# Gated blocks kept as float32 between two stages of a hybrid attention / DeltaNet layer, with a re-measured instruction plan

## The chip, the cores and the metric

The kernel runs on one core of a Trainium2 chip. A core has a matrix engine (PE, whose weight loads are listed apart as PEld), a vector engine (DVE), an activation engine (ACT), a general engine (POOL) and 16 DMA engines, fed here from one queue of the sync engine (SP). Each engine runs its own instructions strictly in order and waits on semaphores for the others. The metric is the device time of one execution in microseconds (us).

## The reference

One layer of a flow-matching backbone: modulated RMSNorm, attention and gated DeltaNet heads side by side, an output projection, and a gated MLP with a depthwise convolution of width 3. The change lies in the MLP, which reads

```python
def conv_ffn(h, w_up, conv_w, conv_b, w_down):
    u = depthwise_conv(h @ w_up, conv_w) + conv_b
    gate, val = jnp.split(u, 2, axis=-1)
    return (jax.nn.silu(gate) * val) @ w_down
```

with h of 2048 tokens x 1024, w_up 1024 x 5632, w_down 2816 x 1024, all float32. The layer's result then passes a last RMSNorm.

## The kernel before

The last part of the program (from L1563) does the output projection, the up stage (h @ w_up, convolution, gate) and the down stage (@ w_down). Nothing in it runs in the order in which it is written: the function `flow` is executed once against a recording object (`Plan`, L195, with `Flow`, L2332, for this part), which notes every instruction and what it depends on, gives each a duration from `cost` (L229), simulates the five engines with a greedy list scheduler (`order`, L307) and then issues the instructions in the simulated order (`issue`, L402). From there that order is fixed on each engine; waits are real. All recorded instructions therefore carry one line number, L407, and are told apart by the names of their tiles.

Float32 accuracy on the matrix engine is got by splitting a float32 tile into two float16 halves, a high part (an ACT cast) and a low part (a subtraction of the high part from the original), and by running three float16 products for one (`PAIRS`, L1581; `split`, L1628):

```python
def split(lo_e, hi, lo, src):
    S.copy(out=hi, in_=src)
    lo_e.tensor_tensor(out=lo, in0=src, in1=hi, op=ALU.subtract)
```

On top of it, up and down products use a 2 x 2 block scheme with seven products in place of eight (Strassen's, in Winograd's form). The operands of the seven products are blocks and combinations of blocks: A11, S2, S1, A12, S3, A22, S4 on the weight side and B11, T2, T1, B21, T3, T4, B22 on the token side.

**Up stage.** 22 column blocks j, each for two halves of the tokens (sb 0 and 1), make 44 steps. A step has seven products of 12 matmuls (`P1` to `P7`, L1954 to L1986), summed in three PSUM banks: ua, ub and uc. The bank ub is read three times in a step (once as u, twice as a row of the tile xa), and the next product that adds to ub may start only once DVE has read it: these are the waits of "PE ub" for "DVE xa". When a step's rows are complete, `after` (L2003) runs the convolution: per row one ACT instruction and two DVE scalar_tensor_tensor instructions on the tile cv, so four of those stand together on DVE; then SiLU on ACT and the gating product on DVE. Blocks B11, T1 come from the column blocks 0 to 10, and T2, T3, B21, B22, T4 are formed when the partner block j + 11 is done. Each of the seven 128 x 512 results is split (`stored`, L1998), with the low part on DVE or POOL, and its float16 pair goes to the DRAM tensor hidc. For the next j, `scales` (L1747) and `parts_of` (L1787) prepare the weights ws_u out of raw_u: seven splits with the low part on POOL, two sums on DVE and two on POOL.

**Down stage.** 14 entries e (seven products, two token halves), each of 4 x 33 matmuls pdn on the 11 pairs hid. `load_hid` (L2058) reads an entry's pairs with two DMA transfers, two entries ahead, into four rotating tiles `ol`. `prep` (L2074) reads w_down (rd), combines up to four blocks of it on DVE and splits them (wd) for the next product; the sums usum, the residual xp / xq and the norm sums nacc_f are DVE work, too, and `last_norm` (L2240) writes finished tokens (fin).

Of the kernel before, what the change touches and what calls it, by code (L numbers as in the profile page):

```python
# [180 lines left out]
class Planned:  # L181
    def __init__(self, eng):
        self.eng, self.calls, self.dur, self.move, self.turns = eng, [], 0.0, 0.0, False
        self.deps, self.behind, self.allocs = set(), set(), []
# [10 lines left out]
class Plan:  # L195
    LAG = dict(PE=200.0, S=250.0, V=170.0, G=170.0, SY=60.0)
    TILE = 14.0
    ISSUED, SEEN = 1275.0, 930.0
# [63 lines left out]

    def add(self, eng, fn, name, kw):
# [38 lines left out]
        op.dur += d  # L302
        op.move, op.turns = max(op.move, a), "transpose" in name and eng == "SY"
# [3 lines left out]
    def order(self, weights):  # L307
# [28 lines left out]
        moved = 0.0  # L336
# [14 lines left out]
        for _ in range(n):  # L351
# [24 lines left out]
            start[i], free[e], end[i] = t, t + o.dur, t + o.dur  # L376
# [48 lines left out]
def kernel(  # L425
# [23 lines left out]
    hidc = dram.tile([2, 7, P, NJ // 2, 2, 512], F16, name="hidc")  # L449
# [1127 lines left out]
    CVW, DTAIL = 1544, ("T1", "T2", "T3", "T4", "B22")  # L1577
# [17 lines left out]
    def flow(plan):  # L1595
# [7 lines left out]
        hidd = plan.wrap(hidc, [2, 7, P, HJ, 2, 512], F16)  # L1603
# [7 lines left out]
        tailc = kept([P, 5, HJ, 2], F16, "tailc")  # L1611
# [175 lines left out]
        def parts_of(j):  # L1787
# [16 lines left out]
            G.tensor_tensor(out=a21, in0=a11, in1=a21, op=ALU.subtract)  # L1804
# [5 lines left out]
            G.tensor_tensor(out=a12, in0=a12, in1=s, op=ALU.subtract)  # L1810
# [187 lines left out]
        def stored(sb, n, j, lo_e, src, z):  # L1998
            z = z.bitcast(F16).rearrange("p (f t) -> p f t", f=2)
            split(lo_e, z[:, 0], z[:, 1], src)  # L2000
            SY.dma_start(out=hidd[sb, BLK.index(n), :, j], in_=z)

        def after(s):  # L2003
# [20 lines left out]
            if not high:  # L2024
                b11, b12 = held[sb] = hold(sb, m)
                V.tensor_tensor(out=b11, in0=c[:, lo], in1=v[:, lo], op=ALU.mult)
# [4 lines left out]
                stored(sb, "B11", m, V, b11, c[:, 0:512])  # L2031
                V.tensor_tensor(out=b11, in0=b12, in1=b11, op=ALU.subtract)
                stored(sb, "T1", m, G, b11, c[:, 512:1024])
                yield
                return
            t1, t3 = held[sb]
# [4 lines left out]
            V.tensor_tensor(out=t1, in0=b22, in1=t1, op=ALU.subtract)  # L2041
            yield
            stored(sb, "T2", m, G, t1, v[:, 1032:1544])
            V.tensor_tensor(out=t3, in0=b22, in1=t3, op=ALU.subtract)
            stored(sb, "T3", m, G, t3, mk(s3, [P, 512], F32, "junk", f"zt3_{m}_{sb}", 1))
            stored(sb, "B21", m, V, b21, c[:, 0:512])
            yield
            V.tensor_tensor(out=b21, in0=b21, in1=t1, op=ALU.subtract)
            stored(sb, "B22", m, V, b22, c[:, 512:1024])
            stored(sb, "T4", m, V, b21, c[:, 1024:1536])  # L2050
# [7 lines left out]
        def load_hid(e):  # L2058
            if e >= len(entries):
                return  # L2060
            p, sb = entries[e]
            n = ORDER[p][1]
            hids[e] = []
            for a, w in ((0, 8), (8, HJ - 8)):
                t = mk(ol3, [P, 8, 2, 512], F16, "ol", f"hid_{e}_{a}", 4)[:, 0:w]
                SY.dma_start(out=t, in_=hidd[sb, BLK.index(n), :, a:a + w])
                if not sb and n in DTAIL:
                    V.tensor_copy(out=t[:, :, :, 511], in_=tailc[:, DTAIL.index(n), a:a + w, :])
                hids[e] += [t[:, j] for j in range(w)]
# [49 lines left out]
        def tails():  # L2119
            e5 = kept([P, 5, HJ], F32, "ends5")  # L2120
# [5 lines left out]
            split(V, tailc[:, :, :, 0], tailc[:, :, :, 1], e5)  # L2126
# [49 lines left out]
        for n, (j, sb) in enumerate(steps):  # L2176
# [15 lines left out]
            elif (j, sb) == (NJ - 1, 0):  # L2192
                drain(work)
                work = scale_wd()
            elif (j, sb) == (NJ - 1, 1):
                drain(work)
                load_hid(0)
                work = prep(0)
# [19 lines left out]
        load_hid(1)  # L2218
# [45 lines left out]
        for e, (p, sb) in enumerate(entries):  # L2264
# [3 lines left out]
            load_hid(e + 2)  # L2268
# [139 lines left out]
```

## Time and profile before

| | us |
|---|---|
| median of 3 runs | 3285.61 (3281.2 to 3290.55) |
| the profiled execution, its own time | 3282.11 |
| its span, first to last instruction | 3280.3 |
| PE busy, of the span | 3073.7 |
| DVE busy | 2407.5 |
| ACT busy | 1775.7 |
| POOL busy | 1722.1 |
| the first up product starts at | 1960.7 |
| the up products give way to the down products at | 2867 |
| the down products end at | about 3267 |

Three places are worked on below: 1960 to 2867 us (up), the boundary around 2867 us, and 2867 to 3267 us (down). A row of the view of waits says which engine stood still for which. A row of the groups of instructions gives count, busy time and mean duration of one, then how long the engine had been idle before them. A row of the windows gives, for a stretch of time, the busy time and number of instructions of PE, PEld, DVE, ACT and POOL, the granted PE clock, and the busy share of the DMA engines with their GB/s.

### The profile page before, as it was taken

The numbers are of one execution on the slowest core, as the hardware profiler recorded it, in microseconds if no ns is written. First come the engines' busy times: TensorE is split into PE (matmuls) and PEld (weight loads), VectorE is DVE, ScalarE is ACT, GpSimd is POOL, SyncE is SP. The second block draws the span as 40 slices with busy tenths as digits, with TensorE's granted clock in tenths as the row PEclk, the third lists the DMA queues.
The fourth block names the chain that finished last, engine by engine and source line by source line (L and its number), as shares of the span: only waits on it lengthen the run. The fifth ranks groups of instructions, "written<-read, shape, count | busy, mean of one in ns | idle before, by whom it ended". The sixth has DMA issues, their size and how long they took to land. (4 is left out here: it accounts for less than half of the span.)

```text
span 3280.3 us, 63243 instructions
## 1 busy us (share of the span) xinstructions
PE 3073.7 (94%) x25298; PEld 1961.1 (60%) x25298; DVE 2407.5 (73%) x3610; ACT 1775.7 (54%) x2947; POOL 1722.1 (52%) x1351
## 2 busy tenths in 40 slices
PE   6899999978999999999997998999999999999998
PEld 3789978865667777777774543444444444444445
DVE  5766486877877777788875688887887888863455
ACT  4534234346787777777776455555555555541211
POOL 4786465555887776776776344554554555200000
PEclk8899999988999999999998999999999999999999
DMA  6322344671112222333325464222222222585696
GB/s 240 91 69 88 109 129 126 177 197 36 55 44 75 67 82 82 105 118 109 104 67 219 178 246 144 74 84 90 90 89 92 93 85 75 186 302 195 234 308 209
DMA packets 280328, 423.65 MB, mean 129 GB/s; under 512 B 23144, under 2 KB 167112, under 8 KB 276944
## 3 DMA queue, kind: packets, MB, share of 16 engines
q1 hardware_dynamic: 278080, 414.19, 37.7%
q0 software_dynamic: 1952, 5.42, 0.6%
q8 instruction: 198, 3.24, 0.4%
q14 instruction: 98, 0.80, 0.1%
HBM read 284.15 MB, written 135.81 MB: 128 GB/s over the span
## 5 line engine op out<-in xcount | busy, mean ns | idle before, releaser
L407 POOL TENSOR_TENSOR lp<-p,hp 128x1024 f16<-128x1024 f32 x288 | 620.4, 2162 | 208.2 <-DVE hp L407 83.3
L407 PEld LDWEIGHTS <-ws_u 128*128 128x128 f16 x3696 | 365.0, 99 | 491.6 <-issue 73.4
L407 DVE TENSOR_REDUCE mx<-sm 128x2 f32<-128x1024 f32 (+1 forms) x320 | 356.4, 1114 | 94.7 <-PE sm L407 91.5
L407 PE MATMUL pdn<-hid,wd 128*128 128x512 f16 (+1 forms) x1980 | 400.8, 365 | 0.0
L407 ACT ACTIVATE p<-sc 128x1024 f32<-128x1024 f32 x288 | 295.2, 1025 | 127.6 <-PE sc L407 123.7
L407 DVE SCALAR_TENSOR_TENSOR cv<-xa,ufw,cv 128x1025 f32<-128x1025 f32 (+1 forms) x176 | 284.6, 1664 | 56.5 <-ACT cv L407 56.2
L407 PEld LDWEIGHTS <-wd 128*128 128x128 f16 x1980 | 193.8, 98 | 204.7
L407 PE MATMUL sc<-q,kh 128*128 128x512 f16 x576 | 220.6, 383 | 6.3 <-ACT p L407 5.9
L407 PE MATMUL sc<-qx,kx 128*128 128x512 f16 x576 | 220.3, 383 | 0.0
L407 POOL TENSOR_TENSOR ws_u<-raw_u,ws_u 128x512 f16<-128x512 f32 x110 | 191.2, 1754 | 50.5 <-ACT ws_u L407 50.5
L407 POOL TENSOR_TENSOR cv<-hold,cv 128x512 f16<-128x512 f32 x44 | 61.3, 1393 | 274.3 <-ACT cv L407 252.5
L407 ACT CAST hp<-p 128x1024 f16<-128x1024 f32 x192 | 201.0, 1047 | 3.7
L407 POOL TENSOR_TENSOR nrc_f<-nrc_f,mhalf 128x8 f32<-128x8 f32 x3 | 4.9, 1636 | 360.3 <-DVE nrc_f L407 360.3
L407 PE MATMUL ops<-vst,hp 128*128 128x65 f16 (+1 forms) x4608 | 191.9, 193 | 1.3 <-ACT hp L407 1.1
L407 PE MATMUL ua<-blk_a,ws_u 128*128 128x512 f16 x792 | 181.7, 379 | 0.7 <-ACT s L407 0.7
L407 PEld LDWEIGHTS <-hp 128*128 128x128 f16 x4608 | 164.9, 97 | 21.0 <-issue 6.9
L407 PE MATMUL po<-ol,ws_o 128*128 128x512 f16 x768 | 175.1, 385 | 1.0 <-DVE ws_o L407 1.0
L407 PE MATMUL ub<-blk_T,ws_u 128*128 128x512 f16 x528 | 129.4, 397 | 29.2 <-DVE xa L407 29.2
L531 PE MATMUL pg<-hl,ws_g 128*128 128x512 f32 x384 | 152.8, 398 | 0.0
L533 PE MATMUL pg<-hl,ws_g 128*128 128x512 f32 x384 | 152.3, 397 | 0.0
L532 PE MATMUL pg<-hl,ws_g 128*128 128x512 f32 x384 | 151.7, 395 | 0.0
L407 ACT CAST t<-pa 128x512 f16<-128x512 f32 x216 | 124.6, 583 | 43.2 <-PE pa L407 39.4
(713 smaller groups left out, 7916.4 us busy)
## 6 DMA issues: line engine op xcount, KB each, us to landing
rd<-in_wd SPq DMA_DIRECT2D x70, 512.0 KB
hidc<-cv SPq DMA_DIRECT2D x132, 256.0 KB
hid<-hidc SPq DMA_DIRECT2D x14, 2048.0 KB
raw_u<-in_wu SPq DMA_DIRECT2D x44, 512.0 KB
tk<-gsc SPq DMA_DIRECT2D x34, 512.0 KB
tT<-gsc SPq DMA_DIRECT2D x66, 256.0 KB
wm<-in_wm SPq DMA_DIRECT2D x64, 256.0 KB
gsc<-kd SPq DMA_DIRECT2D x64, 256.0 KB
```

The source lines that it names most:

```text
L407: fn(**{k: v.get() if isinstance(v, Lazy) else v for k, v in kw.items()})
L531: PE.matmul(out=ps, lhsT=hi_l(k), rhs=hi_r(k), start=st, stop=False)
L532: PE.matmul(out=ps, lhsT=hi_l(k), rhs=lo_r(k), start=False, stop=False)
L533: PE.matmul(out=ps, lhsT=lo_l(k), rhs=hi_r(k), start=False, stop=en)
```

## The change

1. **Storage.** hidc holds the seven blocks as float32 (same bytes). `stored` no longer splits; it writes one, two or three neighbouring blocks with one transfer. The up stage loses 154 ACT casts, 88 low parts on DVE and 66 low parts on POOL, and its transfers into hidc go from 154 to 88. T2, T3 and T4 are now written into the cv tile and go out together.
2. **Down stage.** `load_hid` becomes a generator that brings an entry in six pieces (five of two blocks, one of one) into two landing places, which lie in the unused part of the second `ol` tile, and splits each: one ACT cast and one DVE subtraction, 128 x 1024 for five pieces and 128 x 512 for the sixth. It runs one entry ahead. The last-column corrections (tailc) are patched piecewise in float32.
3. **Weights.** The two sums of `parts_of` that POOL did go to DVE (44 instructions of 128 x 512).
4. **Plan.** The last plan gets other fixed costs (150 ns on DVE and 140 ns on ACT, formerly 65 and 50, and 60 for 65 where a DVE instruction takes a scalar from a tile) and a rule by which a DVE and a POOL instruction that both work on SBUF with at least 128 elements slow each other down to 0.58 of their speed. `prep(0)` and the first `load_hid` start at other steps.

The core of the diff:

```diff
-    hidc = dram.tile([2, 7, P, NJ // 2, 2, 512], F16, name="hidc")
+    hidc = dram.tile([2, 7, P, NJ // 2, 512], F32, name="hidc")
...
+            d, port = o.dur, self.PORT
+            if o.port:
+                x = "G" if e == "V" else "V"
+                over = max(0.0, ported[x] - t)
+                d = d / port if d / port <= over else d + (1.0 - port) * over
+                if over:
+                    free[x] = max(free[x], ported[x] + (1.0 / port - 1.0) * min(over, d))
+                ported[e] = t + d
+            start[i], free[e], end[i] = t, t + d, t + d
...
-            G.tensor_tensor(out=a21, in0=a11, in1=a21, op=ALU.subtract)
+            V.tensor_tensor(out=a21, in0=a11, in1=a21, op=ALU.subtract)
...
-            G.tensor_tensor(out=a12, in0=a12, in1=s, op=ALU.subtract)
+            V.tensor_tensor(out=a12, in0=a12, in1=s, op=ALU.subtract)
...
-        def stored(sb, n, j, lo_e, src, z):
-            z = z.bitcast(F16).rearrange("p (f t) -> p f t", f=2)
-            split(lo_e, z[:, 0], z[:, 1], src)
-            SY.dma_start(out=hidd[sb, BLK.index(n), :, j], in_=z)
+        def stored(sb, n, j, src):
+            i = DBLK.index(n)
+            k = src.shape[1] // 512
+            SY.dma_start(out=hidd[sb, i:i + k, :, j].rearrange("n p t -> p n t"), in_=src.rearrange("p (n t) -> p n t", n=k))
...
-            hids[e] = []
-            for a, w in ((0, 8), (8, HJ - 8)):
-                t = mk(ol3, [P, 8, 2, 512], F16, "ol", f"hid_{e}_{a}", 4)[:, 0:w]
-                SY.dma_start(out=t, in_=hidd[sb, BLK.index(n), :, a:a + w])
+            t = [mk(ol3, [P, 8, 2, 512], F16, "ol", f"hid_{e}_{a}", 4) for a in range(2)]
+            hids[e] = [t[j // 8][:, j % 8] for j in range(HJ)]
+            for i, j0 in enumerate(range(0, HJ, 2)):
+                w = min(2, HJ - j0)
+                a = 3 + 2 * (i % 2)
+                land = t[1][:, a:a + w].rearrange("p j f t -> p (j f t)").bitcast(F32).rearrange("p (j t) -> p j t", j=w)
+                SY.dma_start(out=land, in_=hidd[sb, DBLK.index(n), :, j0:j0 + w])
...
+                split(V, o[:, :, 0, :], o[:, :, 1, :], land)
...
-            load_hid(e + 2)
+            coming = load_hid(e + 1)
...
+    plan.fixed = (150, 60, 0, 140, 42)
```

**DVE in the up stage, around one convolution.** This is the second token half of column block 5, which is a low block. Names: cv is the convolution's pair of tiles, xa the rows read out of PSUM, ws_u and raw_u the weights of the next block in the making, rows and hold places for gated blocks. Before:

```order
L407 TENSOR_TENSOR ws_u_1_32915<-raw_u_1_32768 128x512
L407 SCALAR_TENSOR_TENSOR cv_1_0_32917<-xa,ufw_32259,cv_1_0_32917 128x1025
L407 SCALAR_TENSOR_TENSOR cv_1_1_32920<-xa,ufw_32259,cv_1_1_32920 128x1025
L407 SCALAR_TENSOR_TENSOR cv_1_0_32917<-xa,ufw_32259,cv_1_0_32917 128x1025
L407 SCALAR_TENSOR_TENSOR cv_1_1_32920<-xa,ufw_32259,cv_1_1_32920 128x1025
L407 TENSOR_TENSOR ws_u_1_32915<-ws_u_1_32915,raw_u_0_32729 128x512
L407 TENSOR_TENSOR ends<-cv_1_0_32917,cv_1_1_32920 128x1
L407 TENSOR_TENSOR hold_32978<-cv_1_0_32917,cv_1_1_32920 128x512
L407 TENSOR_TENSOR rows<-cv_1_0_32917,cv_1_1_32920 128x512
L407 TENSOR_TENSOR xa<-ub_0_32817,s_16_0_32830 128x512
```

And now:

```order
L422 SCALAR_TENSOR_TENSOR cv_1_0_32733<-xa,ufw_32115,cv_1_0_32733 128x1025
L422 SCALAR_TENSOR_TENSOR cv_1_1_32735<-xa,ufw_32115,cv_1_1_32735 128x1025
L422 SCALAR_TENSOR_TENSOR cv_1_0_32733<-xa,ufw_32115,cv_1_0_32733 128x1025
L422 SCALAR_TENSOR_TENSOR cv_1_1_32735<-xa,ufw_32115,cv_1_1_32735 128x1025
L422 TENSOR_TENSOR ws_u_1_32789<-raw_u_1_32572 128x512
L422 TENSOR_TENSOR ends<-cv_1_0_32733,cv_1_1_32735 128x1
L422 TENSOR_TENSOR cv_1_0_32733<-cv_1_0_32733,cv_1_1_32735 128x512
L422 TENSOR_TENSOR rows<-cv_1_0_32733,cv_1_1_32735 128x512
L422 TENSOR_TENSOR xa<-ub_0_32633,s_16_0_32646 128x512
```

The first weight sum (ws_u out of raw_u alone) has moved from ahead of the four convolution instructions to behind them, and the second (ws_u out of ws_u and raw_u) to behind the read of ub.

**POOL at the same place**, the low parts and sums of that weight block, before:

```order
L407 TENSOR_TENSOR ws_u_0_32913<-raw_u_0_32729,ws_u_0_32913 128x512
L407 TENSOR_TENSOR raw_u_1_32768<-raw_u_0_32729,raw_u_1_32768 128x512
L407 TENSOR_TENSOR ws_u_0_32913<-ws_u_1_32915,ws_u_0_32913 128x512
L407 TENSOR_TENSOR ws_u_0_32913<-raw_u_0_32729,ws_u_0_32913 128x512
L407 TENSOR_TENSOR ws_u_1_32915<-raw_u_1_32768,ws_u_1_32915 128x512 x2
L407 TENSOR_TENSOR raw_u_0_32729<-raw_u_0_32729,ws_u_1_32915 128x512
L407 TENSOR_TENSOR ws_u_0_32913<-ws_u_1_32915,ws_u_0_32913 128x512
L407 TENSOR_TENSOR ws_u_1_32915<-raw_u_0_32729,ws_u_1_32915 128x512
```

And now:

```order
L422 TENSOR_TENSOR ws_u_0_32750<-raw_u_0_32407,ws_u_0_32750 128x512 x2
L422 TENSOR_TENSOR ws_u_0_32750<-ws_u_1_32789,ws_u_0_32750 128x512
L422 TENSOR_TENSOR ws_u_1_32789<-raw_u_1_32572,ws_u_1_32789 128x512
L422 TENSOR_TENSOR ws_u_0_32750<-ws_u_1_32789,ws_u_0_32750 128x512
L422 TENSOR_TENSOR ws_u_1_32789<-raw_u_1_32572,ws_u_1_32789 128x512
L422 TENSOR_TENSOR ws_u_1_32789<-raw_u_0_32407,ws_u_1_32789 128x512
```

The two raw_u sums are gone from POOL; its third instruction now reads the weight sum (ws_u_1_32789) that DVE makes behind the four convolution instructions.

**SP's queue in the down stage**, where entry 11 is loaded and the weights of the last product (rd) stream in. Before:

```order
L407 DMA hid_0_38215<-hidc 128x8192
L407 DMA rd_4_1_38218<-in_wd 128x4x256
L407 DMA out<-fin_3_38049 128x3x511
L407 DMA out<-fin_3_38049 128x3x1
L407 DMA hid_8_38236<-hidc 128x3072
```

And now:

```order
L422 DMA hid_1_38003<-hidc 128x1024 x2
L422 DMA rd_4_1_38023<-in_wd 128x4x256
L422 DMA x1c<-xq_37885 128x512
L422 DMA xp_38030<-x1c 128x3x512
L422 DMA rd_6_1_38046<-in_wd 128x4x256
L422 DMA out<-fin_3_37801 128x3x511
L422 DMA out<-fin_3_37801 128x3x1
L422 DMA out<-fin_6_37991 128x2x511
L422 DMA out<-fin_6_37991 128x2x1
L422 DMA hid_1_38003<-hidc 128x1024
L422 DMA xq_38097<-x1c 128x512
L422 DMA hid_1_38003<-hidc 128x1024
```

Two large transfers have become six, of which two start at once and the others stand between weights, residuals and output, each behind the split that empties its landing place.

More of the change, by code (lines that the diff above doesn't have):

```diff
@@ L183, in __init__ @@
         self.eng, self.calls, self.dur, self.move, self.turns = eng, [], 0.0, 0.0, False
-        self.deps, self.behind, self.allocs = set(), set(), []
+        self.deps, self.behind, self.allocs, self.port = set(), set(), [], False
 class PlanEngine:
@@ L261, in cost, with shares @@
         return 46 + n * 1.05, 0.0
+    @staticmethod
+    def shares(eng, name, kw):
+        if eng not in "VG" or name.startswith("dma_start") or name in ("tensor_reduce", "memset"):
+            return False
+        return not any(isinstance(x, Lazy) and x.root.psum for x in kw.values()) and int(np.prod(kw["out"].shape[1:])) >= 128
     def add(self, eng, fn, name, kw):
@@ L302, in add @@
         op.dur += d
+        op.port = self.shares(eng, name, kw)
         op.move, op.turns = max(op.move, a), "transpose" in name and eng == "SY"
@@ L335, in order @@
         free = dict.fromkeys(self.LAG, 0.0)
-        moved = 0.0
+        moved, ported = 0.0, dict(V=0.0, G=0.0)
         pool = {e: [] for e in free}
@@ L1602, in flow @@
         h2 = [plan.wrap(h2c[i], [P, KT, 512], F32) for i in range(NCH)]
-        hidd = plan.wrap(hidc, [2, 7, P, HJ, 2, 512], F16)
+        hidd = plan.wrap(hidc, [2, 7, P, HJ, 512], F32)
         spare = plan.wrap(rows, [P, R_END], F32)
@@ L1610, in flow @@
         ogate = kept([P, KT], F32, "ogate")
-        tailc = kept([P, 5, HJ, 2], F16, "tailc")
+        tailc = kept([P, 5, HJ], F32, "tailc")
         ends = kept([P, 4, HJ], F32, "ends")
@@ L2024, in after @@
             if not high:
-                b11, b12 = held[sb] = hold(sb, m)
-                V.tensor_tensor(out=b11, in0=c[:, lo], in1=v[:, lo], op=ALU.mult)
+                t1, b12 = held[sb] = hold(sb, m)
+                b11 = c[:, lo]
+                V.tensor_tensor(out=b11, in0=b11, in1=v[:, lo], op=ALU.mult)
                 V.tensor_tensor(out=b12, in0=c[:, hi], in1=v[:, hi], op=ALU.mult)
@@ L2030, in after @@
                 yield
-                stored(sb, "B11", m, V, b11, c[:, 0:512])
-                V.tensor_tensor(out=b11, in0=b12, in1=b11, op=ALU.subtract)
-                stored(sb, "T1", m, G, b11, c[:, 512:1024])
+                stored(sb, "B11", m, b11)
+                V.tensor_tensor(out=t1, in0=b12, in1=b11, op=ALU.subtract)
+                stored(sb, "T1", m, t1)
                 yield
                 return
-            t1, t3 = held[sb]
+            t1, b12 = held[sb]
             b21, b22 = v[:, lo], v[:, hi]
@@ L2119, in tails @@
         def tails():
-            e5 = kept([P, 5, HJ], F32, "ends5")
+            e5 = tailc
             V.tensor_tensor(out=e5[:, 0], in0=ends[:, 1], in1=ends[:, 0], op=ALU.subtract)
@@ L2294, in flow @@
                                               stop=k == HJ - 1 and f == 2, skip_group_check=True)
+                        next(coming, None)
                         if c0 == 0:
@@ L2343, in cost @@
             return Plan.cost(eng, name, kw, rate, fixed)
-    flow(Flow(tc, psn, pt3, ps3))
+    plan = Flow(tc, psn, pt3, ps3)
+    plan.fixed = (150, 60, 0, 140, 42)
+    flow(plan)
     p3.close()
```

33 lines of the change are left out of this document (15 added, 18 removed).

## The prediction

> **What bounds the kernel now.** I read the windows first, by stage, then the chain of waits, then who kept PE waiting. The windows are the start of the up stage, its steady part, its end, and the down stage (columns: window, length, then busy us and count of PE, PEld, DVE, ACT, POOL, then PE clock, DMA share, GB/s):
>
> ```profile
> 1960.50:2042.00 81.50, 70.93 (x333) 32.26 (x332) 68.20 (x80) 45.84 (x71) 33.61 (x20) 0.94 0.40 139
> 2042.00:2760.00 718.00, 671.57 (x3313) 306.03 (x3311) 595.30 (x782) 408.68 (x703) 374.50 (x238) 0.98 0.25 87
> 2760.00:2867.00 107.00, 100.06 (x457) 45.07 (x458) 88.32 (x121) 53.12 (x91) 33.22 (x21) 0.97 0.44 150
> 2867.00:3268.00 401.00, 400.03 (x2013) 197.53 (x2011) 205.47 (x311) 94.93 (x140) 9.14 (x6) 1.00 0.74 255
> ```
>
> In the down stage PE is never idle, at full clock: nothing can be won there, only lost. The chain of waits gives PE's real pace, and the windows of the tiles ua, ub, uc (PE's count first) and uns say how much there was to do:
>
> ```profile
> 2867.11 265.47 PE pdn L407 x1230
> ...
> 2042.00:2760.00 718.00, 196.45 (x857) 40.74 (x71) 0.98 0.25 87
> ...
> 2042.00:2760.00 718.00, 303.40 (x1284) 71.25 (x105) 0.98 0.25 87
> ...
> 2042.00:2760.00 718.00, 187.64 (x840) 47.81 (x70) 0.98 0.25 87
> ...
> 2042.00:2760.00 718.00, 17.67 (x332) 6.08 (x36) 4.00 (x36) 0.98 0.25 87
> ```
>
> 265.47 / 1230 = 0.2158 us per matmul. The steady part holds 857 + 1284 + 840 = 2981 of them (ua, ub, uc), 643.3 us of work, and 17.7 us of weight norms (uns): 661.0 of 718 us. So **57 us are lost**. PE's waits there:
>
> ```profile
> PE ub L407 <- DVE xa L407: 34.6, 15, 2.9
> PE uns L407 <- ACT junk L407: 9.5, 9, 2.1
> PE ub L407 <- POOL ws_u L407: 1.7, 1, 1.7
> ```
>
> 45.8 us are waits; the other 11 (671.57 busy less 661.0) are products at less than full pace, in a part whose clock averages 0.98. What makes xa late is seen in the timeline around the longest wait (start, duration, what):
>
> ```profile
> 2424.94 1.16 POOL L407 TENSOR_TENSOR ws_u<-raw_u,ws_u 128x512 f16<-128x512 f32 x1 [2.81 <-ACT ws_u L407]
> 2426.06 1.28 POOL L407 TENSOR_TENSOR raw_u<-raw_u,raw_u 128x512 f32<-128x512 f32 x1
> 2427.73 1.71 POOL L407 TENSOR_TENSOR ws_u<-ws_u,ws_u 128x512 f16<-128x512 f32 x1 [0.39 <-ACT ws_u L407]
> 2429.40 6.33 POOL L407 TENSOR_TENSOR ws_u<-raw_u,ws_u 128x512 f16<-128x512 f32 x3
> ...
> 2426.04 8.68 DVE L407 SCALAR_TENSOR_TENSOR cv<-xa,ufw,cv 128x1025 f32<-128x1025 f32 x4 [0.97 <-ACT cv L407]
> 2434.64 1.64 DVE L407 TENSOR_TENSOR ws_u<-ws_u,raw_u 128x512 f32<-128x512 f32 x1
> ...
> 2436.88 1.75 DVE L407 TENSOR_TENSOR rows<-cv,cv 128x512 f32<-128x512 f32 x1
> 2438.55 0.68 DVE L407 TENSOR_TENSOR xa<-ub,s 128x512 f32<-128x512 f32 x1
> ...
> 2433.62 2.75 PE L407 MATMUL ub<-blk_b,ws_u 128*128 128x512 f16 x12
> 2439.28 2.96 PE L407 MATMUL ub<-blk_T,ws_u 128*128 128x512 f16 x7 [2.90 <-DVE xa L407]
> ```
>
> While POOL works through six low parts and sums, four convolution instructions take 8.68 us. They are slower beside POOL, as the groups say (up stage first, then the down stage, where POOL is still):
>
> ```profile
> L407 DVE SCALAR_TENSOR_TENSOR cv<-xa,ufw,cv 128x1025 f32<-128x1025 f32 x84 | 147.4, 1797 | 24.5 <-ACT cv L407 24.2
> L407 DVE TENSOR_TENSOR cv<-cv,cv 128x512 f16<-128x512 f32 x63 | 74.9, 1205 | 0.9
> ...
> L407 DVE SCALAR_TENSOR_TENSOR cv<-xa,ufw,cv 128x1025 f32<-128x1025 f32 x4 | 4.9, 1274 | 0.0
> L407 DVE TENSOR_TENSOR cv<-cv,cv 128x512 f16<-128x512 f32 x3 | 2.0, 681 | 0.0
> ```
>
> Alone the four would take 4 x 1.274 = 5.1 us. Behind them stood a weight sum and a gating product, and only then the read of ub.
>
> **The change, part by part.** *Storage.* 88 low parts leave DVE: at 0.681 us alone, 60 us, at 1.205 beside POOL, 106. The 44 weight sums come, 30 us alone. DVE is therefore lighter by 30 to 76 us of the 752 (68.20 + 595.30 + 88.32) it was busy. ACT loses 154 casts; it delayed PE in the uns row only. POOL loses 66 low parts and 44 sums:
>
> ```profile
> L407 POOL TENSOR_TENSOR ws_u<-raw_u,ws_u 128x512 f16<-128x512 f32 x100 | 177.5, 1790 | 41.8 <-ACT ws_u L407 41.8
> L407 POOL TENSOR_TENSOR ws_u<-ws_u,ws_u 128x512 f16<-128x512 f32 x40 | 66.8, 1670 | 3.5 <-ACT ws_u L407 3.5
> L407 POOL TENSOR_TENSOR cv<-hold,cv 128x512 f16<-128x512 f32 x42 | 58.5, 1392 | 243.8 <-ACT cv L407 239.4 <-DMA hidc<-cv 4.4
> L407 POOL TENSOR_TENSOR raw_u<-raw_u,ws_u 128x512 f32<-128x512 f32 x20 | 32.4, 1620 | 6.2 <-POOL ws_u L407 4.8 <-DVE ws_u L407 1.4
> L407 POOL TENSOR_TENSOR raw_u<-raw_u,raw_u 128x512 f32<-128x512 f32 x20 | 28.1, 1407 | 5.9 <-DVE ws_u L407 4.5 <-POOL ws_u L407 1.4
> L407 POOL TENSOR_TENSOR zt<-hold,zt 128x512 f16<-128x512 f32 x11 | 17.2, 1562 | 0.0
> L407 POOL TENSOR_TENSOR zt<-rows,zt 128x512 f16<-128x512 f32 x10 | 15.9, 1588 | 0.2 <-POOL cv L407 0.2
> ```
>
> The last five go: 152.1 of 396.4 us, 38%.
>
> *Order.* More than the share counts where POOL's work falls. In the new order the third POOL instruction of a weight block needs a sum that DVE makes behind the four convolution instructions, so POOL can disturb these with two instructions, not six. Each of the six cost DVE (8.68 - 5.1) / 6 = 0.6 us; with two the four take about 6.3. Behind them stand a weight sum and two products of 0.68 and ends (0.15): 8.5 to 9.5 us from the start to the read of ub, as POOL resumes there, against 12.5 before (2438.55 - 2426.04). The saving of 3 to 4 us exceeds the longest wait, 2.90. I put the xa waits at 6 us of 34.6 (bounds: none, and 21.4, if they shrink only with POOL's share), the slow products at 3 of 11 (0 to 7), since they follow the waits, and the uns and POOL waits at 7 of 11.2, since ACT is lighter (bounds 0 and 11.2). Gain in the steady part: 28.6 + 8 + 4 = **40 us**, between 17 and 57.
>
> *Start of the up stage.* Its token blocks are split by ACT and DVE as before; PE is idle for 81.5 - 70.93 = 10.6 us, which the change touches only through the first steps' storage: 2 us, 0 to 8.
>
> *Boundary.* Entry 0's six splits and those of entry 1 come on top of the last steps, where DVE is busy 88.32 of 107 us. Their prices are those of the weight splits of the same shape:
>
> ```profile
> L407 DVE TENSOR_TENSOR wd<-rd,wd 128x1024 f16<-128x1024 f32 x15 | 18.1, 1221 | 8.6 <-ACT wd L407 8.6
> L407 ACT CAST wd<-rd 128x1024 f16<-128x1024 f32 x15 | 15.4, 1044 | 63.4 <-PE pdn L407 28.0 <-DVE rd L407 19.8 <-DMA x1c<-xq 14.5
> ```
>
> An entry costs DVE 5 x 1.22 + 0.68 = 6.8 us and ACT about 5.8. I charge 2 us (0 to 10): the last steps shed their own low parts.
>
> *Down stage.* 14 x 6.8 = 95 us more DVE work: 205.47 becomes 300 of 401 us. PE's matmuls cover it; uncovered it would cost all 95. The cover is thinnest under the last two weight sets:
>
> ```profile
> 2980.00:3040.00 60.00, 60.00 (x279) 27.18 (x278) 18.24 (x27) 9.58 (x14) 0.00 (x0) 1.00 0.54 194
> ...
> 3152.00:3210.00 58.00, 58.00 (x278) 27.43 (x277) 36.37 (x56) 8.33 (x11) 1.64 (x1) 1.00 0.98 329
> ```
>
> 36.37 + 2 x 6.8 = 50 of 58 us for DVE, and a DMA share of 0.98. The six transfers pass SP's queue behind residuals and output that themselves wait for DVE. I charge 3 us (0 to 15).
>
> Sum: 40 + 2 - 2 - 3 = **37 us** off the profiled execution's 3282.1, which is 3.5 below the median of the runs; off the median 3285.6 that is 3248.6, so 3248.
>
> **Rivals.** *E, all of it goes.* If POOL's remaining instructions never meet the convolutions, and ACT's waits go too, the whole 57 us return: 3285.6 - 57 = 3229. For it: the saving per convolution exceeds every wait. Against: 154 low parts stay on POOL. The Trainium skill (SBUF — State Buffer, "Who interferes with whom") says that a DVE instruction with two SBUF inputs and a GpSimd instruction that reads SBUF exclude each other for their whole length. By that rule the four and two of POOL's 1.16 us would take 5.1 + 2.3 = 7.4 us; the rows agree only roughly, since four and six would be 12.1 where 8.68 was measured.
>
> *B, only the share counts.* POOL's low parts meet other convolutions instead; xa waits fall to 21.4, slow products to 7, ACT's waits stay: 13.2 + 4 = 17 us less 4 below, 3272.5. For it: the other four-instruction group of each pair of steps has POOL beside it too. The Trainium skill speaks for this side (Perfetto Trace Analysis, "Optimizing Scalar/DVE Operations"): offloading between GPSIMD and DVE might not help, since they share a read port; then the 44 moved sums give nothing and 13.2 becomes 8.
>
> *C, it does not do what it says.* The plan's better durations do not hold on the chip, waits move elsewhere: 0, 3285.6. For it: PE's order of products stays almost the same.
>
> *D, slower: the two landing places.* A pair of pieces must land and be split before the next pair may start: three rounds per entry, 28.5 us (4 x 33 x 0.2158), so 9.5 us a round. In the DMA-heavy entries a 512 KB piece takes 1.6 us at 329 GB/s; behind six rd transfers as large, plus its own pair and two splits (2.4 us), a round is 6 x 1.6 + 3.2 + 2.4 = 15 us, and an entry late by 3 x 15 - 28.5 = 17 us; with four such entries (under the three- and four-term weight sets) 68 us. Less the gain of 42, the kernel would be 26 us slower: 3311. It turns slower from (28.5 + 42 / 4) / 3 = 13 us a round. Against: rd is itself held back by its buffers, and 0.54 at 2980 to 3040 leaves room.
>
> **How the numbers follow.** Forecast 0.55, own range 3236 to 3262; E 0.13; B 0.15; C 0.07; D 0.10. No change means within 0.3% (10 us), which a measurement of this kernel can hardly tell. Faster: 0.55 + 0.13 + 0.11 of B = 0.79; same: 0.04 of B and C = 0.11; slower 0.10. The range 3228 to 3282 leaves out D, most of C and what lies beyond E.
>
> **What would show it.** Right: in the steady part the xa waits under 10 us, four convolutions together at 6 to 7 us, PE clock 1.00, POOL busy near 40% less; no wait of PE for hid or wd after the boundary. Wrong: xa waits above 20 us (B), or PE waits for "DVE hid" or "DMA hid" of over 20 us in all (D), or waits for POOL's ws_u, if its low parts, begun later, reach the next step late.

## The result, and the profile after

| | before | changed |
|---|---|---|
| median of 4 runs, us | 3283.40 (3280.45 to 3290.55) | 3207.22 (3206.38 to 3210.48) |
| ratio, 95% interval | | 0.9767 (0.9748 to 0.9785) |
| span of the profiled execution, us | 3280.3 | 3205.2 |
| first up product starts, us | 1960.7 | 1953.6 |
| last down product starts, us | 3266.8 | 3191.9 |

The kernel is 76 us faster. 37 were forecast (3248, range 3228 to 3282), so the direction was right and the gain twice as large as said. From the first up product to the last down product it took 1306.1 us and takes 1238.3: 67.8 us of the gain lie there. The other 7.1 us lie ahead of it.

The windows of the changed kernel: start of the up stage, its steady part, its end, the down stage (columns as before):

```profile
1953.60:2026.00 72.40, 57.23 (x265) 25.92 (x264) 62.44 (x66) 37.98 (x58) 25.50 (x12) 0.88 0.43 150
2026.00:2700.00 674.00, 673.81 (x3410) 311.57 (x3409) 511.21 (x781) 355.43 (x596) 219.46 (x153) 1.00 0.28 97
2700.00:2797.00 97.00, 96.91 (x451) 43.97 (x450) 83.02 (x110) 49.51 (x80) 12.28 (x8) 1.00 0.50 163
2797.00:3193.00 396.00, 395.20 (x1991) 195.31 (x1988) 280.90 (x400) 158.46 (x206) 6.52 (x4) 1.00 0.77 256
```

In the steady part PE is busy for 673.81 of 674 us at full clock, where it was busy for 671.57 of 718. The end of the stage, where 7 of 107 us had been idle, is full too, and the down stage still is, with DVE at 281 us in place of 205. Only the start still has idle time, 15 us. The view of who kept PE waiting, from 1950 us to the end (three rows of the norms' small products, 1.2 to 1.6 us each, are left out):

```profile
PE ub L422 <- ACT blk_b L422: 7.4, 1, 7.4
PE ub L422 <- DVE blk_b L422: 2.5, 1, 2.5
PE ua L422 <- ACT s L422: 1.9, 1, 1.9
...
PE ub L422 <- DVE xa L422: 1.4, 1, 1.4
...
PE ub L422 <- DVE u L422: 0.6, 1, 0.6
PE uns L422 <- ACT junk L422: 0.2, 1, 0.2
```

The row of before, over the whole program, was

```profile
PE ub L407 <- DVE xa L407: 38.8, 18, 2.9
```

Waits for xa went from 38.8 us in 18 places to 1.4 in one, at the start of the up stage; there is none for hid or wd. The timeline at the convolution that the prediction showed, the second token half of column block 5, which now comes at 2389 us:

```profile
2389.38 6.69 DVE L422 SCALAR_TENSOR_TENSOR cv<-xa,ufw,cv 128x1025 f32<-128x1025 f32 x4 [1.17 <-ACT cv L422]
2391.11 3.87 POOL L422 TENSOR_TENSOR ws_u<-raw_u,ws_u 128x512 f16<-128x512 f32 x2 [5.12 <-ACT ws_u L422]
...
2395.99 0.68 DVE L422 TENSOR_TENSOR ws_u<-raw_u 128x512 f32<-128x512 f32 x1
2396.59 0.15 DVE L422 TENSOR_TENSOR ends<-cv,cv 128x1 f32<-128x1 f32 x1
2396.66 0.68 DVE L422 TENSOR_TENSOR cv<-cv,cv 128x512 f32<-128x512 f32 x1
...
2397.26 0.68 DVE L422 TENSOR_TENSOR rows<-cv,cv 128x512 f32<-128x512 f32 x1
2397.39 1.56 POOL L422 TENSOR_TENSOR ws_u<-ws_u,ws_u 128x512 f16<-128x512 f32 x1 [2.42 <-PE ua L422]
2397.86 0.68 DVE L422 TENSOR_TENSOR xa<-ub,s 128x512 f32<-128x512 f32 x1
```

The four convolution instructions take 6.69 us beside two of POOL's, and xa is read 8.5 us after their start (2397.86 - 2389.38), where it was 12.5. The down stage's new work is in the groups of DVE and ACT between 2797 and 3193 us:

```profile
L422 DVE TENSOR_TENSOR hid<-hid,hid 128x1024 f16<-128x1024 f32 x49 | 59.6, 1222 | 23.8 <-ACT hid L422 23.7
L422 ACT CAST hid<-hid 128x1024 f16<-128x1024 f32 x62 | 64.4, 1042 | 74.5 <-DVE hid L422 42.6 <-DMA hid<-hidc 32.0
```

### The profile page after: what moved, and what is told of

Its sections match the earlier page's. It is cut to its first block, busy times and chain, and to the rows that moved or that the text cites. A ratio compares the mean times of both kernels' runs of the same rounds, so it can differ in the third digit from the quotient of the medians.

```text
span 3205.2 us, 62953 instructions
## 1 busy us (share of the span) xinstructions
PE 3049.6 (95%) x25298; PEld 1954.9 (61%) x25298; DVE 2387.5 (74%) x3669; ACT 1769.9 (55%) x2876; POOL 1532.4 (48%) x1241
## 4 chain that ended last, share of the span: by engine, by line
PE 76%; DVE 10%; POOL 5%; DMA 3%; issue 3%; ACT 3%; SPq 0%; POOLq 0%; DVEq 0%; ACTq 0%
PE pdn L422 12%; PE ub L422 10%; PE sc L422 7%; PE uc L422 7%; PE ua L422 6%; PE ops L422 6%; PE po L422 6%; PE sm L422 3%; PE pa L422 2%; PE pg L547 1%; PE pg L546 1%; PE pg L548 1%; PE pw L422 1%; DVE mx L422 1%; PE pz L422 1%
## 5 line engine op out<-in xcount | busy, mean ns | idle before, releaser
L422 ACT ACTIVATE p<-sc 128x1024 f32<-128x1024 f32 x288 | 295.0, 1024 | 127.3 <-PE sc L422 123.6
L422 DVE SCALAR_TENSOR_TENSOR cv<-xa,ufw,cv 128x1025 f32<-128x1025 f32 (+1 forms) x176 | 254.9, 1501 | 48.8 <-ACT cv L422 48.7
L422 POOL TENSOR_TENSOR ws_u<-raw_u,ws_u 128x512 f16<-128x512 f32 x110 | 176.4, 1615 | 138.4 <-ACT ws_u L422 114.6
L422 POOL TENSOR_TENSOR usg<-usg,mhalf 128x3 f32<-128x3 f32 x22 | 19.1, 867 | 276.8 <-DVE usg L422 276.8
L422 PE MATMUL sm<-kh,q 64*128 64x512 f16 (+1 forms) x320 | 119.0, 372 | 18.5 <-DVE mx L422 18.3
```

The source lines that it names most:

```text
L422: fn(**{k: v.get() if isinstance(v, Lazy) else v for k, v in kw.items()})
```

## Experiments

Every median below stands beside runs of the kernel before on the same chip, whose medians were 3282.9 to 3285.1. "Stretch" means the time from the start of the first up product to the start of the last down product, from the profiled execution.

### Which part carries it

Theory 1: the order of the instructions carries the gain. Theory 2: the lighter load on DVE, POOL and ACT carries it. The changed kernel with the old plan:

```diff
-        PORT = 0.58
...
-    plan.fixed = (150, 60, 0, 140, 42)
```

> The changed kernel with the old plan (fixed costs 65, 65, 50 and no rule for DVE beside POOL); storage and weight sums as changed. Theory 1 (the order counts: POOL may disturb the convolutions with only two instructions because its third needs a sum made behind them): the old plan puts the first weight sum ahead of the convolutions again, so waits of PE ub for DVE xa of 15 us or more return in the up stage, about 3230 to 3245. Theory 2 (less work on DVE, POOL and ACT is cover enough, whatever the order): xa waits stay below 5 us and the time is within 10 us of the changed kernel, 3207 to 3217.

The kernel before with the new plan (those lines added, and the rule's code):

> The kernel before with the new plan alone (fixed costs 150, 60, 140 and the 0.58 rule); float16 storage and POOL's weight sums as before. Theory 1: the order carries the gain, so at least 25 of the 76 us come, 3258 or less. Theory 2: the same work is to be done beside the convolutions, so 10 us or less, 3273 or more, xa waits near the 34.6 us of before.

The changed kernel with the weight sums on POOL again:

```diff
-            V.tensor_tensor(out=a21, in0=a11, in1=a21, op=ALU.subtract)
+            G.tensor_tensor(out=a21, in0=a11, in1=a21, op=ALU.subtract)
...
-            V.tensor_tensor(out=a12, in0=a12, in1=s, op=ALU.subtract)
+            G.tensor_tensor(out=a12, in0=a12, in1=s, op=ALU.subtract)
```

> The changed kernel with the two weight sums on POOL again, storage and plan as changed. Theory 1: POOL gets back two instructions that do not hang on a DVE sum behind the convolutions, xa waits of 10 us or more and 3220 to 3235. Theory 2: POOL is 90 us lighter than before anyway, and DVE lighter still, so within 8 us of the changed kernel, 3207 to 3215.

Both edits together, so that storage alone is changed:

> Storage as changed (float32 blocks, split beside the down products), with the old plan and POOL's weight sums: part 1 and 2 of the change alone. Theory 1: only POOL's share counts, as in my rival B, 17 us and no more than 30, so 3253 to 3270. Theory 2: the cover suffices, 50 us or more come from it alone, 3233 or less, xa waits below 10 us.

Plan and sums changed, storage as before:

> The kernel before with the whole new plan and the weight sums on DVE, but float16 storage with its splits in the up stage. Theory 1 (the order carries the gain and the sums on DVE keep POOL from the convolutions): at least 5 us better than the plan alone (3228.7), so 3224 or less. Theory 5 (with 88 low parts still on it DVE, at 721 of 810 us, is the bound of the up stage by now): 44 sums of 0.7 to 1 us more on DVE make it slower than the plan alone, 3230 to 3270.

| storage | sums on DVE | plan | median, us | ratio (95%) | stretch, us | PE ub for DVE xa, us |
|---|---|---|---|---|---|---|
| before | no | old | 3283.4 | | 1306.1 | 38.8 |
| new | no | old | 3274.2 | 0.9967 (0.9953 to 0.9981) | 1300.3 | 47.2 |
| new | yes | old | 3248.8 | 0.9888 (0.9873 to 0.9903) | 1270.1 | 31.3 |
| before | no | new | 3228.7 | 0.9827 (0.9812 to 0.9842) | 1254.9 | 5.2 |
| before | yes | new | 3232.3 | 0.9838 (0.9824 to 0.9853) | 1257.4 | 7.3 |
| new | no | new | 3214.9 | 0.9783 (0.9769 to 0.9798) | 1241.1 | 1.7 |
| new | yes | new | 3207.2 | 0.9767 (0.9748 to 0.9785) | 1238.3 | 1.4 |

In these runs "plan" means the fixed costs and the rule; the other starting steps of `prep(0)` and of the first `load_hid` go with the storage.

Theory 2 falls as it was put. Storage alone takes 154 splits out of the up stage and gains 10 us; its waits for xa even rise. The plan alone, with every split still in the up stage, gains 55. The sums gain 25 us under the old plan and 8 under the new one beside the new storage; beside the old storage they gain nothing (3232.3 against 3228.7, where PE's waits for POOL's ws_u rise from 4.3 to 10.3 us). Theory 1 is not the whole either. Under the old plan storage and sums together gain some 35 us, and two of its expectations missed: with the sums on POOL again the waits for xa are 1.7 us and not 10 or more, and plan and sums beside the old storage give 3232.3 and not 3224 or less. Storage alone and the old plan each came out 4 us slower than even theory 1 had them.

How the same waits come from the order shows at one place of the run with the old plan and all the changed work (the timeline; the places from 2065 to 2683 us are alike):

```profile
2449.01 0.69 DVE L422 TENSOR_TENSOR ws_u<-raw_u 128x512 f32<-128x512 f32 x1 [0.23 <-ACT raw_u L422]
...
2451.24 7.57 DVE L422 SCALAR_TENSOR_TENSOR cv<-xa,ufw,cv 128x1025 f32<-128x1025 f32 x4
2452.35 1.19 POOL L422 TENSOR_TENSOR ws_u<-ws_u,ws_u 128x512 f16<-128x512 f32 x1 [1.57 <-ACT ws_u L422]
2453.50 6.33 POOL L422 TENSOR_TENSOR ws_u<-raw_u,ws_u 128x512 f16<-128x512 f32 x3
2458.74 1.64 DVE L422 TENSOR_TENSOR ws_u<-ws_u,raw_u 128x512 f32<-128x512 f32 x1
...
2461.50 0.68 DVE L422 TENSOR_TENSOR xa<-ub,s 128x512 f32<-128x512 f32 x1
...
2462.23 2.75 PE L422 MATMUL ub<-blk_T,ws_u 128*128 128x512 f16 x12 [1.49 <-DVE xa L422]
```

There the first weight sum stands ahead of the convolutions again, POOL gets three instructions in between (the fourth ends behind them), and xa is read 10.3 us after their start: PE waits 1.49 us. With 12.5 us it waited 2.90, with 8.5 not at all. In the run with the plan alone, at the place of column block 5:

```profile
2404.21 6.68 DVE L422 SCALAR_TENSOR_TENSOR cv<-xa,ufw,cv 128x1025 f32<-128x1025 f32 x4 [1.11 <-ACT cv L422]
...
2405.90 3.91 POOL L422 TENSOR_TENSOR ws_u<-raw_u,ws_u 128x512 f16<-128x512 f32 x2 [5.07 <-ACT ws_u L422]
...
2410.81 0.68 DVE L422 TENSOR_TENSOR ws_u<-raw_u 128x512 f32<-128x512 f32 x1
...
2411.62 1.67 POOL L422 TENSOR_TENSOR raw_u<-raw_u,raw_u 128x512 f32<-128x512 f32 x1 [1.82 <-issue]
...
2413.77 0.68 DVE L422 TENSOR_TENSOR xa<-ub,s 128x512 f32<-128x512 f32 x1
```

Here too the first weight sum stands behind the convolutions, and only two POOL instructions run beside them. The third is a sum that POOL still does in this run; it overwrites a block of raw_u that the DVE sum reads, so it must wait for that one (the run with the fixed costs alone names the wait at this place: 1.76 us for DVE ws_u). xa is read 9.6 us after the start, and PE does not wait. At the places between these (column blocks 11 and up) POOL had kept away already before: 5.1 to 5.3 us for the four and 7.6 to 9.4 to the read, now 5.1 and 7.0 to 7.2. Storage alone goes the other way; its groups of convolutions in the up stage (from 1980 us), ahead of them the 1025-wide one of before:

```profile
L407 DVE SCALAR_TENSOR_TENSOR cv<-xa,ufw,cv 128x1025 f32<-128x1025 f32 x80 | 142.3, 1823 | 23.9 <-ACT cv L407 23.6
...
L422 DVE SCALAR_TENSOR_TENSOR cv<-xa,ufw,cv 128x1025 f32<-128x1025 f32 x80 | 171.0, 2192 | 19.1 <-ACT cv L422 19.1
L422 DVE SCALAR_TENSOR_TENSOR cv<-xa,ufw,cv 128x1024 f32<-128x1024 f32 x88 | 112.0, 1323 | 25.8 <-ACT cv L422 25.8
```

POOL's weight work has gathered beside the 1025-wide convolutions (2192 ns each), and the waits for xa are 47.2 us.

### Which part of the plan

Theory 3: the fixed costs; theory 4: the 0.58 rule. On the kernel before, each alone; then the changed kernel without the rule:

> The kernel before with only the three fixed costs of the last plan changed (150, 60, 140), no rule for DVE beside POOL; the plan with both had given 56 us of the 76. Theory 3 (the true price of each instruction is what the plan lacked: some ten small weight-norm instructions stood ahead of the read of ub as if nearly free): at least 35 of the 56 come, 3250 or less. Theory 4 (the rule that makes DVE and POOL slow each other carries it): less than 20, 3265 or more.

> The kernel before with only the 0.58 rule in the last plan, the fixed costs as before. Theory 3: less than 20 us, 3265 or more. Theory 4: at least 35 of the 56 us, 3250 or less, with xa waits of PE below 10 us.

> The changed kernel with the new fixed costs but without the 0.58 rule in the plan. On the kernel before, the rule was worth 23 us on top of the fixed costs (3252.0 to 3228.7), and there it took away the waits of the weight norms for ACT. Here POOL has 38% less to do and DVE and ACT less too. If the rule is needed with the lighter engines too: 3220 or more. If the slack of the lighter engines has taken its place: 3207 to 3215.

The fixed costs alone: 3252.0 us, 0.9898 (0.9882 to 0.9915), 31 us gained. The rule alone: 3274.6, 0.9971 (0.9960 to 0.9983), 9. Together 55: neither theory has it whole. With the fixed costs alone, PE's waits in the last part are

```profile
PE uns L422 <- ACT junk L422: 18.3, 8, 3.7
PE ub L422 <- DVE xa L422: 16.9, 9, 4.0
```

and with the rule added they fall to none and 5.2. The place of column block 5 shows one thing that the fixed costs do and the rule alone does not: with them the first weight sum stands behind the convolutions (6.70 us for the four, 9.6 to the read of ub), with the rule alone six POOL instructions still run beside them (9.3 and 12.6). What the costs stand for can be read from the groups of before (up stage, DVE and ACT):

```profile
L407 DVE TENSOR_TENSOR bet<-usg 128x1 f32<-128x1 f32 x20 | 3.2, 158 | 0.4
...
L407 ACT CAST ws_u<-raw_u 128x512 f16<-128x512 f32 x97 | 57.2, 613 | 8.3 <-POOL raw_u L407 5.3 <-PE ua L407 2.0 <-PE uc L407 0.8
```

The old plan priced the first at 65 + 1 / 0.96 = 66 ns and the second at 50 + 42 + 512 x 0.836 = 520, the new one at 151 and 610. The new costs agree with these durations, and in that sense they are measured. They do not agree with the pace, because the end of an instruction overlaps the next one: in the timeline of the changed kernel above, DVE instructions of 0.68 us start 0.60 us apart (old price 598 ns, new 683), and ACT casts of 614 ns that stand back to back start 520 ns apart (medians before). The old plan therefore did not take DVE and ACT for faster than they are. The new one takes them for slower, by some 85 to 90 ns an instruction, and finds the better order; why it does is not shown.

In the changed kernel the rule is worth little: 3214.0 (0.9792, 0.9777 to 0.9806) against 3207.2, and nothing of it in the up and down stages, as the stretch without it is 1238.4 and with it 1238.3. Some 3 us lie at the head of the out-projection, where PE's waits for oraw are 12.2 us without it and 6.2 with it, while those for ol, osg and junk_o are 2.2 and 8.0, so what shortens it is open; 3.6 lie in a part ahead that has the same instructions in both. Beside the new storage and sums the up and down stages no longer need the rule. The same rule in every planned part of the program:

```diff
-    ISSUED, SEEN, PORT = 1275.0, 930.0, 1.0
+    ISSUED, SEEN, PORT = 1275.0, 930.0, 0.58
```

> The changed kernel with the 0.58 rule in every planned part of the program, not in the last alone. If true prices help wherever a plan sets the order: faster by 5 to 30 us in the parts before 1769 us, 3177 to 3202. If those parts are bound elsewhere: 3207 within 10, and either sign.

3231.7 us (0.9846, 0.9832 to 0.9861), 24 slower than the changed kernel and outside both answers: the out-projection's products start at 1787.2 in place of 1762.5 us, its up stage waits are those of the changed kernel. In the parts ahead, whose prices had been set without the rule, it costs; by what is not shown.

### Is it POOL at all?

Theory H1: POOL's work beside the convolutions makes the reads of ub late. H2: DVE's own order does. All engines in the order of before, but POOL's float16 low parts in the last part become memsets, so that these low parts are zero and the result leaves them out:

```diff
+                    if self.silent and self.ops[i].eng == "G" and "in1" in kw and kw["out"].dtype == F16:
+                        self.tc.nc.gpsimd.memset(kw["out"].get(), 0.0)
+                        continue
```

> The kernel before, every engine's instructions in exactly the order of before, but in the last part of the program each float16 low part that POOL computes (weights and hidden blocks) is a memset of the same tile, which reads nothing; so the low parts are zero and the output differs. It leaves order alone and takes most of POOL's work away from the side of the convolutions. Theory H1 (POOL's contention makes the reads of ub late, as the prediction has it): four convolution instructions take 5.1 us nearly everywhere, xa waits fall below 10 us, and the time is 3250 or less. Theory H2 (what stands ahead of the read of ub in DVE's fixed order makes it late; contention is secondary): xa waits stay above 20 us, 3265 or more.

> The changed kernel in its own order with the same memsets in place of POOL's low parts. H1 and H2 both: PE already waits for nearly nothing in the steady part, so 3200 to 3209; more than 10 us less than 3207 would mean that contention still costs PE time that the waits do not show.

3196.8 us (0.9738, 0.9723 to 0.9752): the old order, with the old storage, the old plan and POOL quiet, is faster than the changed kernel. No wait for xa and none for ACT junk is left. At the convolution of column block 5 the four take 5.06 us beside five memsets, and ub is read 6.9 us after their start, with DVE's order as it was when it took 12.5. That decides for H1. The windows of the up stage, of before and then of this run:

```profile
1960.70:2867.00 906.30, 842.35 (x4100) 383.27 (x4099) 751.62 (x980) 507.50 (x863) 441.33 (x277) 0.98 0.29 99
```

```profile
1955.20:2780.00 824.80, 820.15 (x4098) 378.86 (x4097) 614.28 (x981) 509.42 (x865) 201.01 (x277) 1.00 0.32 109
```

The same DVE instructions (980 and 981) take 137 us less. 213 low parts are replaced in this window (145 of weights, 64 of hidden blocks, 4 of token blocks), so each had cost DVE about 0.64 us on average. The groups of that run:

```profile
L411 DVE SCALAR_TENSOR_TENSOR cv<-xa,ufw,cv 128x1025 f32<-128x1025 f32 x88 | 113.9, 1336 | 24.6 <-ACT cv L411 17.4 <-DMA raw_n<-in_wd 5.5 <-DMA raw_u<-in_wu 1.4
...
L409 POOL MEMSET ws_u<- 128x512 f16 x145 | 71.1, 525 | 8.9 <-PE ua L411 8.9
```

The changed kernel with the same memsets takes 3200.9 (0.9750, 0.9734 to 0.9767), 6 us less than 3207.2. With POOL quiet the change as a whole is thus worth nothing (3200.9 against 3196.8): what it gains, it gains by getting out of POOL's way. A memset also shortens POOL's own chain, and whether zeros change PE's pace is not separated; so a second test was made with real work: the seven low parts of each weight block on DVE, nothing left out. Here the plan orders anew, so the order is not held.

```diff
-                split(G, w[i // 4][:, i % 4, 0], w[i // 4][:, i % 4, 1], x)
+                split(V, w[i // 4][:, i % 4, 0], w[i // 4][:, i % 4, 1], x)
```

> The kernel before, its old plan and storage, with all seven low parts of each weight block on DVE; nothing left out. POOL keeps the hidden blocks' low parts and the two sums. With the silent POOL DVE was busy 610 of 820 us; plus 105 that is 715. If sharing costs (H1): most of the 86 us come back, 3200 to 3240, although DVE has more work than before. If the memset run gained through POOL's and ACT's shorter chains: DVE, with 105 us more, falls behind, 3280 or more.

> The changed kernel with all seven low parts of each weight block on DVE in place of POOL; nothing left out. DVE in the up stage was busy 657 of 843 us; it sheds some 40 us of slower convolutions and 15 of slower sums (as with the silent POOL, 609 of 820) and gets 154 x 0.68 = 105 us, 710 of 828. If sharing with POOL is what costs: 3195 to 3207. If DVE's own load is by now the limit: xa waits come back, 3215 to 3260.

On the kernel before: 3231.7 us (0.9846, 0.9823 to 0.9869), 51 gained by one letter, with 154 more instructions on the busiest helper engine; waits for xa 5.5 us. On the changed kernel: 3213.1 (0.9794, 0.9766 to 0.9821), between the two answers. Its windows show how little the added DVE work adds (138 instructions more in this window, 83 us at the 0.60 us that each takes back to back); first that run, then the changed kernel:

```profile
1960.00:2790.00 830.00, 810.95 (x4045) 374.53 (x4043) 658.86 (x1074) 431.59 (x715) 32.29 (x26) 0.99 0.32 107
```

```profile
1960.00:2790.00 830.00, 814.54 (x4061) 375.33 (x4059) 645.08 (x936) 434.77 (x720) 251.99 (x171) 0.99 0.31 107
```

13.8 us more DVE time, because its convolutions are back at 1283 ns (1680 in the changed kernel). Of the 6 us that it is slower, 3.4 lie in the stretch (1241.7 against 1238.3), at its start: one wait for xa of 7.9 us before 2010 us, none later. The rest lies ahead of the up stage. Two versions that keep a part on POOL, `V if n in ("S1", "S2", "S3", "S4") else G` and `G if j in (0, HJ) else V`, and the changed kernel beside the second:

> The changed kernel with four of the seven low parts of each weight block (S1 to S4, the sums) on DVE, three on POOL. H1 with room on DVE: between the changed kernel and the one with all seven on DVE, 3198 to 3207. If DVE's load costs by the instruction: slower than the changed kernel by some 5 us or more.

> The changed kernel with all seven low parts on DVE, except those of the first two weight blocks, which stay on POOL, since they are formed beside the end of the out-projection and the start of the up stage. If the 6 us of the run with all of them on DVE lie at the start alone: its 7.9 us wait goes and the time is 3202 to 3208, level with the changed kernel or just below. If DVE's load costs everywhere: 3211 to 3217.

> The changed kernel itself once more, beside the other run on the same chip: 3207 within 3.

3207.8 (3202.7 to 3209.5), 3208.4 (3206.4 to 3213.4) and 3208.8 (3206.6 to 3210.3): level. The 7.9 us wait is gone in the second, whose stretch is 1238.4. No version that does all the work beats the changed kernel by more than can be measured; PE has no idle time left but at the start.

### The landing places (rival D)

```diff
-                a = 3 + 2 * (i % 2)
+                a = 3
```

> The changed kernel with one landing place for the float32 pieces in place of two, so that a piece can start only when the one before is split. By rival D of the prediction (transfers stand behind six weight transfers, 9.6 us, and their own 1.6 us, and a split of 2.4 us: 13.6 us a piece, 82 us for an entry that has 28.5) four entries would be late by 53 us each and the time above 3400. If the time from the issue of a piece to its second split stays near the 4 to 6 us seen with little traffic, six take 24 to 36 us and the time is 3207 to 3240. If the cover is wide and pieces are early, nothing: 3207 within 5.

3231.0 us (0.9837, 0.9822 to 0.9852), 24 slower than the changed kernel; the middle answer. PE's waits between 2780 and 3220 us, and the window with the longest:

```profile
PE pdn L422 <- ACT hid L422: 11.0, 3, 8.4
PE pdn L422 <- DVE hid L422: 3.8, 4, 1.4
```

```profile
3080.00:3140.00 60.00, 49.52 (x225) 22.67 (x224) 50.95 (x74) 18.64 (x24) 3.21 (x1) 0.91 1.02 320
```

So the landing places are the right place to look: one costs where the DMA engines are full (1.02 in this window), two suffice. D's price, 15 us a round and 13.6 us a piece in the expectation here, was too high: with one place 82 us an entry would have followed, and the whole down stage lost 20.

## Why the prediction was right and wrong

**What bounds the kernel.** Right: PE's lost time in the up stage was nearly all that could be won, and the down stage, though DVE's load there rose by 75 us, lost nothing.

**The cause.** Right, and better borne out than the forecast trusted, but its price was too low. The forecast put 0.6 us on each POOL instruction, (8.68 - 5.1) / 6. Rows of single instructions at column block 5 of the changed kernel show how the two engines meet:

```profile
2391.11 1.76 POOL L422 TENSOR_TENSOR ws_u<-raw_u,ws_u 128x512 f16<-128x512 f32 x1 [5.12 <-ACT ws_u L422]
2391.77 2.19 DVE L422 SCALAR_TENSOR_TENSOR cv<-xa,ufw,cv 128x1025 f32<-128x1025 f32 x1
2392.84 2.13 POOL L422 TENSOR_TENSOR ws_u<-raw_u,ws_u 128x512 f16<-128x512 f32 x1
2393.89 2.18 DVE L422 SCALAR_TENSOR_TENSOR cv<-xa,ufw,cv 128x1025 f32<-128x1025 f32 x1
```

They take turns. The ends are 2392.87 (POOL), 2393.96 (DVE), 2394.97 (POOL) and 2396.07 (DVE): each instruction ends 1.0 to 1.1 us after the other engine's, and the time in which it only stood counts in its duration. Before, 72 of the 73 convolution instructions in the up stage that took over 1.5 us end 1.08 to 1.09 us after a POOL instruction of 128 x 512. By the number of POOL instructions that end while the four run, the four take 4.9 to 5.1 us (none), 6.68 (two), 7.57 (three), 8.67 (four) and 9.68 (five), as medians over the changed kernel, before, storage alone, plan alone and the old plan: 0.9 us each. Of the prediction's six, the first had ended when the four began and the last was served behind them; four were served. The two-instruction place came out nearly as described: four in 6.3 us forecast, 6.69 measured; 8.5 to 9.5 us to the read of ub forecast, 8.5 measured. (Before, two gating products stood ahead of that read, hold and rows, and not one.)

The Trainium skill (SBUF — State Buffer, "Who interferes with whom") says that DVE instructions with two SBUF inputs contend with GpSimd instructions that read SBUF, not with those that only write; the runs agree, as the convolutions take 1283 to 1336 ns beside memsets, and xa<-ub, with one operand in PSUM, about 680 ns in every run. The Trainium skill calls the contention an exclusive lock there. The prediction found its rows to agree with that only roughly, because it counted six instructions for four; the turns above agree, at 0.9 us in place of the 1.16 that a low part takes alone.

All signs that the prediction names for being right came: no wait for xa in the steady part, four at 6.7 us, clock 1.00, POOL's busy share there 38% lower, no wait for hid or wd.

**The steady part, 40 us: the step that failed.** It left 6 us of waits for xa, 3 of the 11 us of slow products and 7 of the 11.2 us of waits for ACT and POOL standing, 16 us in all. What was left is 0.2 us of waits, at clock 1.00. The forecast let the waits for xa shrink in part. But the read of ub comes 8.4 to 8.5 us after the start of nearly every 1025-wide group, PE has other products to do until then, and so no place waits. The slow products went with the waits: before, the 12 products behind the wait of 2.90 us took 4.04 us in place of 2.75. The waits of uns for ACT junk are a cost of their own, and their forecast was only too low. Over the program they were 16.0 us before; they fell to 3.9 with storage alone and 3.2 with the rule alone, where the waits for xa rose to 47.2 and 41.4, and they stayed at 18.3 with the fixed costs alone and 11.8 with the low parts on DVE, where those for xa fell to 16.9 and 5.5. With POOL quiet both are gone. What ends them in the changed kernel is not settled. The windows of ua, ub, uc and uns in the steady part of the changed kernel:

```profile
2026.00:2700.00 674.00, 200.76 (x876) 41.83 (x73) 1.00 0.28 97
...
2026.00:2700.00 674.00, 298.95 (x1316) 74.19 (x110) 1.00 0.28 97
...
2026.00:2700.00 674.00, 195.71 (x876) 50.11 (x73) 1.00 0.28 97
...
2026.00:2700.00 674.00, 17.28 (x342) 5.67 (x38) 4.33 (x40) 1.00 0.28 97
```

By the prediction's own ruler that is 3068 x 0.2158 + 17.3 = 679 us of work in 674: its loss fell from 57 us to minus 5 (part of uns overlaps the products, so the ruler was 5 us too long), and the gain is about 62. Rival E, at 0.13, has this outcome for the steady part, and its argument, a saving per convolution that exceeds every wait, held. Its condition did not: POOL's instructions still meet the convolutions, two at each place. Its time, 3229, is 22 us too slow all the same.

**End of the stage and boundary, minus 2.** Wrong sign. The end of the up stage held 10 us of loss, too (3.1 us of waits for xa and 4.0 for ACT junk among it): 445 products and 0.8 us of uns are 96.8 us of work in 107, now 449 products fill 96.9 of 97. The prediction looked there only for a charge.

**Start, plus 2.** Minus 6 by the same ruler (297 products and 0.9 us of uns in 81.3 us, now 230 in 72.4): the wait for ACT blk_b rose from 5.5 to 7.4 us, for DVE blk_b from 1.4 to 2.5, for s from 0.7 to 1.9. **Down stage, minus 3.** 0. **Ahead of the up stage.** Not in the sum: 3 us at the head of the out-projection, which the run without the rule does not have. A further 3.6 us lie where both kernels run the same instructions; that part ended at 1721.1 to 1726.7 us in the profiles of this study, the rule everywhere apart, so they are no gain of the change. The terms as measured, 62 + 10 - 6 + 0 + 3 + 4 = 73, make up nearly all of the 75 us between the two spans.

**What carries it.** The prediction's sum costs storage and sums and lets the plan only place them. The runs turn this round: the plan alone gains 55 us with the work unchanged, storage alone 10. The sentence that POOL is held behind a DVE sum is borne out, but it was credited to the wrong part: the plan alone holds POOL there, with both raw_u sums still on POOL. So the path was right and the part of the change that opens it was not the one in the sum.

**Rival B** did not come: the waits for xa are 1.4 us and not 21.4. That its time (3272.5; its "4 below" is 3 by the terms named) is near that of storage alone (3274.2) is chance, as the waits for xa rose there. The Trainium skill (Perfetto Trace Analysis, "Optimizing Scalar/DVE Operations") says that offloading operations between GPSIMD and DVE might not help. Here moving low parts from POOL to DVE gained 51 us on the kernel before; on the changed kernel, where PE no longer waits in the steady part, it gained nothing. **Rival C** is refuted. **Rival D**: above.

**Open.** Not settled are why the sums on DVE help only beside the new storage, why fixed costs above the pace give the better order, what ends the waits for ACT junk, and what shortens the head of the out-projection.

## What to carry to other kernels

Where an order is planned from prices, try other prices before moving work: three numbers of fixed cost gained 31 us here. When comparing a price with a profile, look at both the duration and the distance from start to start: here the old prices had the second right, the new ones the first. The waits here did not shrink in proportion: where the late result comes before PE has run out of other products, the whole wait goes, so forecast them place by place, and waits for different engines apart. Before shortening a helper's work, ask whether it slows its neighbour: replacing it by something that reads nothing, in the same order, tells it in one run.

## What the runs showed of the hardware that was not expected

A low part of 128 x 512 on POOL (1.16 us alone) takes more time from DVE where it meets two-input work there, 0.9 us, than DVE needs to do it itself, 0.60 back to back; on average over the up stage it took 0.64: of some 83 us moved to DVE in the window, 13.8 appeared in its busy time. Beside each other the two engines took turns, instruction by instruction. A POOL memset of the same tile takes 525 ns and left the convolutions near their lone price. After 8.4 us without products the granted clock was 0.50 for some 5 us, and products stood 427 ns apart in place of 216 (one landing place, 3117 to 3122 us), so a long wait costs more than its own length: with 14.8 us of waits the down stage took 20 us longer (430 against 410).
